# First layer of a four-branch mixer: its start cut into four steps by feature rows, with fp32 modulation weights as the stationary operand

## The chip, the cores and the metric

The kernel runs on one core of one Trainium2 chip. The metric is the device time of one launch in microseconds (us); lower is better. Before the change three runs gave 2394.82, 2383.02 and 2387.49 us: median 2387.49.

## The reference

Two layers (DEPTH = 2) of one mixer work on 1024 latent tokens and 256 context tokens of 1024 features. Cut to the part that the change touches:

```python
shift, scale, gate = jnp.split(c_act @ w_ada[l] + b_ada[l], 3, axis=-1)     # the same with c_ctx for the context
h  = _rmsnorm(x, norm_g[l]) * (1.0 + scale[:, None]) + shift[:, None]
hc = _rmsnorm(xc, norm_g[l]) * (1.0 + scale_c) + shift_c
ckv, krope, u_s5, x_lru, cq, x_pool, gpath, mlogit = jnp.split(h @ w_in[l], IN_SPLITS, axis=-1)
... four token mixers (latent attention, S5, RG-LRU, pooling), gates, merge, w_out ...
x = x + gate[:, None] * y
```

The modulation is a vector-matrix product for two vectors (latent and context) with the 1024 x 2048 part of `w_ada` that holds shift and scale. Every column of every input product needs all 1024 feature rows of `h`, and row k of `h` needs the modulation of feature tile k and the root mean square of its token, which is a sum over all features of `x`.

## The kernel before

Features lie on partitions, tokens on the free axis, in three chunks: 0 (256 context tokens), 1 and 2 (512 latent tokens each). The eight feature tiles of 128 are the index k. Large products run in float32r: `split` makes a high and a low part of each operand (ScalarE copies the rounded high part, VectorE or GpSimd subtracts), and `gemm` runs three passes per k (lo*hi, hi*lo, hi*hi) into one PSUM bank, so a column tile of one chunk costs 24 matmuls.

The start of the first layer (`run`, L1151) follows the steps of the string `START` (L43): load x by chunk (x), squares and root mean squares (q, `stats`), modulation of 256 features (a, `ada_first`, L258), and two input rows of one chunk (b, or p with a part on GpSimd; `build_h`, L314). `ada_first` splits each 128 x 512 piece of `w_ada` into two float32r parts (`wah`, `wal`) and streams them, 256 columns at a time, past a stationary operand of 4 columns (`chl`, both vectors in two parts); the 4 x 256 result is copied out by ScalarE and turned by two transposes, then VectorE adds bias and gain (`ada_end`):

```python
for d in range(2):
    for w in (lo, hi):
        self.mm(pt, self.cact[:, k + d], w[:, 256 * d:256 * d + 256], k + d == 0 and w is lo, k + d == NK - 1 and w is hi)
```

`mla_in` (L345) then multiplies all three chunks by column tiles 0 (`ckv`) and `w_kr` (`krope`), in the banks pg, pg, pS, pS, pS, pm. After it come `mla_kv`, `s5_in` (the first PSUM tile of which is a product of chunk 0 in pg), `lru_in` (L560: column tiles 3 and 4 of all chunks), `cq_in` and the rest.

A scheduler sets the order of each engine's instructions when the kernel is built, by data dependences, by the order of the code and by the priorities that `hp()` raises. On the chip each engine runs its own list in that fixed order, and an instruction that waits holds up all that stand behind it on its engine. All transfers are issued from one queue (SP), also in a fixed order. PSUM pools: `psg` 2 banks, `pss` 3, `psm` 2, `psp` 1; a bank is given again once its last reader is done.

Of the kernel before, what the change touches and what calls it, by code (L numbers as in the profile page):

```python
# [35 lines left out]
SC = 192  # chunk columns of the S5 recurrence: ctx 32, latent 128, ctx again 32  # L36
# [31 lines left out]
class Net:  # L68
# [75 lines left out]
    def rsqrt(self, y, v, t):  # L144
        """y = v ** -0.5 by Newton's steps from the exponent-halving guess."""
# [16 lines left out]
    def load_w(self, src, nk, small=False):  # L162
        """[128, nk * m] stationary columns -> per k the high and low tiles, loaded in parts of at most 512 columns."""
# [28 lines left out]
    def prologue(self):  # L192
# [5 lines left out]
        self.dma(self.ident, I["ident"])  # L198
# [13 lines left out]
        self.qmask = [k[:, 5:6], k[:, 6:7]]  # rows of q without the copies of the rope part  # L212
        self.vec = []
        for l in range(DEPTH):
            a = self.t(pk, f"vec{l}", NV)
            self.dma(a, I["vec"][l])
            self.vec.append(a)
        self.mod = [view(self.t(pk, f"mod{l}", 48), 24, 2) for l in range(DEPTH)]
        cv, t = self.t(pk, "cv", 16), self.sc(16)
        self.cv = view(cv, 8, 2)  # L220
        self.dma(cv, I["cvec"])
        self.act(t, cv, AF.Tanh, scale=0.5)
        self.stt(cv, t, 1.0, cv, ALU.add, ALU.mult)
        ch = view(self.t(pk, "chl", 32, dt=F32R), 8, 4)
        self.split(ch[:, :, 0:2], ch[:, :, 2:4], view(cv, 8, 2))
        self.cact = ch
# [51 lines left out]
    def ada_end(self, l, f, n, pq, rest=None):  # L278
        """Modulation of feature tiles f .. f + n - 1 from its products (the sum of pq and rest): bias, and the norm's gain on 1 + scale."""
# [4 lines left out]
        if rest is not None:  # L284
            self.stt(mo, rest, 0.5, mo, ALU.mult, ALU.add)
# [4 lines left out]
    def stats(self, ci, parts, pool, R):  # L290
        """Reciprocal root mean squares of the tokens of chunk ci, on all partitions of R, from squares [128, n].

        A generator: sums and roots, then the spread to the partitions.
        """
# [16 lines left out]
        self.act(R[:, s0:s0 + n], pr[:, 0:n], AF.Copy)  # L311
        yield

    def build_h(self, l, ci, x, R, ks, pool=False):  # L314
        """Rows ks of the normalised, modulated input of chunk ci (high and low parts)."""
        s0, n = CH[ci]
        who = 1 if ci == 0 else 0
        for k in ks:
# [4 lines left out]
            if pool:  # L323
                self.act(tmp, x[:, k], AF.Identity, scale=A)
                self.tt(tmp, tmp, R[:, s0:s0 + n], ALU.mult, self.nc.gpsimd)
            else:
                self.stt(tmp, x[:, k], A, R[:, s0:s0 + n], ALU.mult, ALU.mult)
# [4 lines left out]
    def tok_sums(self, out, parts, ones):  # L332
        """Sums over features (partitions) of parts [K, n] -> out [128 tokens, n / 128 (, cols)]."""
# [11 lines left out]
    def mla_in(self, l, pa):  # L345
        """Columns ckv and krope, scaled by their norms' gains; sums of squares by token."""
# [989 lines left out]
```

## Time and profile before

| what | value |
|---|---|
| runs: lowest, median, highest | 2383.02, 2387.49, 2394.82 us |
| span of the profiled execution | 2395.9 us |
| TensorE matmul busy over the span | 2303.0 us (96%) |
| VectorE, ScalarE, GpSimd busy | 1585.0, 989.4, 223.3 us |
| moved by DMA | 234.52 MB, mean 98 GB/s |

The page gives no time of the profiled execution beside its span of 2395.9 us, which is its own time here; it lies 8.4 us above the median of the runs. In a row of a timeline the first number is the start in us from the begin of the span, the second the time until the end of the group. Matmuls are pipelined, so their duration holds a latency; how long one occupies the engine is read from one start to the next. A float32 matmul (not float32r) shows as two rows: a group "x8" of 128x2 stands for four matmuls of the program.

### The profile page before, as it was taken

Reading aid. Unit: us, or ns where it says so; the run is one execution under the profiler, and the core shown is the slowest. Engines: PE = TensorE matmul, PEld = TensorE weight load, DVE = VectorE, ACT = ScalarE, POOL = GpSimd, SP = SyncE. Lnnn points to the kernel's source line nnn. Section 1 sums busy time; section 2 is a strip of 40 time slices with the busy share of each in tenths; the row PEclk is TensorE's granted clock in tenths of the full one; section 3 lists DMA queues with packets and bytes.
Section 4 is the critical chain, followed back from the end, with each engine's and each line's share of the span. In section 5 each row is a group of like instructions: output and inputs, shape, how many; then the busy total and the mean of one; then the engine's idle time right before and its main releaser. Section 6 shows DMA issues by size and latency. Waiting matters only on the chain. (4 is left out here: it accounts for less than half of the span.)

```text
span 2395.9 us, 33295 instructions
## 1 busy us (share of the span) xinstructions
PE 2303.0 (96%) x11808; PEld 1883.5 (79%) x11808; DVE 1585.0 (66%) x3533; ACT 989.4 (41%) x1971; POOL 223.3 (9%) x265
## 2 busy tenths in 40 slices
PE   3899999999989999999999999999999999999999
PEld 2687888888778777888888777778888788877887
DVE  6745659766887977445563864679667988864243
ACT  5535656666322222212142444756665322322231
POOL 1200000000000111111112100000000001111110
PEclk8889999999999999999999999999999999999999
DMA  7132241221533324223324423142212431233135
GB/s 248 46 100 67 81 151 55 65 67 49 156 103 99 93 74 126 86 71 111 103 91 132 146 90 110 58 161 70 74 58 80 142 111 49 81 90 102 47 115 158
DMA packets 212455, 234.52 MB, mean 98 GB/s; under 512 B 76352, under 2 KB 138048, under 8 KB 212288
## 3 DMA queue, kind: packets, MB, share of 16 engines
q1 hardware_dynamic: 212288, 232.39, 31.9%
q8 instruction: 93, 1.52, 0.3%
q14 instruction: 74, 0.61, 0.1%
HBM read 173.86 MB, written 58.46 MB: 97 GB/s over the span
## 5 line engine op out<-in xcount | busy, mean ns | idle before, releaser
L139 PE MATMUL pg<-h,wh 128*128 128x512 f32 (+1 forms) x4608 | 1364.1, 377 | 2.9 <-DVE h L124 2.8
L139 PEld LDWEIGHTS pg<-h,wh 128*128 128x128 f32 x4608 | 837.5, 190 | 161.7 <-DVE h L124 5.7
L139 PE MATMUL pg<-h,wl 128*128 128x512 f32 (+2 forms) x2304 | 881.2, 383 | 3.6 <-ACT h L136 3.2
L139 PEld LDWEIGHTS pg<-h,wl 128*128 128x128 f32 (+1 forms) x2304 | 437.4, 190 | 86.1 <-ACT h L136 5.0
L121 DVE TENSOR_TENSOR wl<-wr,wh 128x512 fp32r<-128x512 f32 x268 | 193.2, 723 | 194.6 <-ACT wh L136 193.8
L136 ACT ACTIVATE wh<-wr 128x512 fp32r<-128x512 f32 x268 | 168.2, 628 | 296.5 <-PE pg L139 157.2
L136 ACT ACTIVATE st<-pg 128x512 f32<-128x512 f32 (+1 forms) x200 | 110.7, 554 | 335.9 <-PE pg L139 333.7
L121 POOL TENSOR_TENSOR y<-y,st 128x512 f32<-128x512 f32 (+1 forms) x120 | 151.0, 1258 | 971.4 <-DVE st L124 930.1
L139 PE MATMUL pm<-b,wph 128*128 128x512 f32 (+1 forms) x640 | 185.3, 373 | 1.6 <-DVE b L121 1.6
L136 ACT ACTIVATE P<-pS,sm,qs 128x512 f32<-128x512 f32 (+1 forms) x200 | 138.7, 703 | 48.0 <-DVE sm L128 44.9
L124 DVE SCALAR_TENSOR_TENSOR st<-st,pm 128x512 f32<-128x512 f32 (+1 forms) x120 | 75.5, 630 | 121.4 <-PE pm L139 111.9
L139 PE MATMUL pS<-k,q 128*128 128x512 f32 (+1 forms) x600 | 144.3, 364 | 1.9 <-DVE q L121 1.7
L139 PEld LDWEIGHTS pm<-b,wph 128*128 128x128 f32 x640 | 116.0, 189 | 25.0 <-DVE b L121 3.1
L139 PE MATMUL pP<-pt,v 128*128 128x256 f32 x656 | 127.7, 301 | 3.4 <-DVE pt L121 1.3
L139 PEld LDWEIGHTS pP<-pt,v 128*128 128x128 f32 x656 | 99.6, 188 | 35.9 <-ACT pt L136 22.3
L527 DVE TENSOR_REDUCE sm<-pS 128x1 f32<-128x512 f32 (+1 forms) x200 | 113.3, 586 | 15.8 <-PE pS L139 14.5
L121 DVE TENSOR_TENSOR pt<-pm,pt 128x512 fp32r<-128x512 f32 x164 | 106.9, 682 | 25.0 <-ACT pt L136 24.3
L139 PE MATMUL pm<-b,wpl 128*128 128x256 f32 (+1 forms) x320 | 119.9, 375 | 2.5 <-DVE y L124 1.8
L136 ACT ACTIVATE pt<-pm 128x512 fp32r<-128x512 f32 x164 | 91.2, 600 | 70.6 <-PE pm L142 70.4
L139 PEld LDWEIGHTS pS<-k,q 128*128 128x128 f32 x600 | 98.8, 189 | 19.0 <-ACT P L136 4.3
L142 PE MATMUL pm<-ident,P 128*128 128x128 f32 x656 | 107.1, 274 | 0.2 <-ACT P L136 0.2
L124 DVE SCALAR_TENSOR_TENSOR pP<-wa,cv,pP 128x256 f32<-128x256 f32 x196 | 95.4, 487 | 15.1 <-DMA wa<-in_w_ada 11.0
(240 smaller groups left out, 2637.7 us busy)
## 6 DMA issues: line engine op xcount, KB each, us to landing
wr<-in_w_in SPq DMA_DIRECT2D x196, 256.0 KB, 2.9
wa<-in_w_ada SPq DMA_DIRECT2D x96, 256.0 KB, 2.9
wr<-in_w_out SPq DMA_DIRECT2D x64, 256.0 KB, 3.0
gD<-st SPq DMA_DIRECT2D x32, 256.0 KB, 2.0
tD<-st SPq DMA_DIRECT2D x32, 256.0 KB, 2.1
og<-oD SPq DMA_DIRECT2D x32, 256.0 KB, 2.8
og<-gD SPq DMA_DIRECT2D x32, 256.0 KB, 3.1
wr<-in_w_branch SPq DMA_DIRECT2D x64, 128.0 KB, 2.1
```

The costliest lines, as they stand in the source:

```text
L121: (eng or self.nc.vector).tensor_tensor(out=out, in0=a, in1=b, op=op)
L124: self.nc.vector.scalar_tensor_tensor(out=out, in0=a, scalar=s, in1=b, op0=op0, op1=op1)
L136: self.nc.scalar.activation(out=out, in_=a, func=func, scale=scale, **kw)
L139: self.nc.tensor.matmul(out=out, lhsT=lhsT, rhs=rhs, start=start, stop=stop)
L142: self.nc.tensor.transpose(out=out, in_=in_, identity=ident)
L527: nc.vector.tensor_reduce(out=mx3[:, i:i + 1], in_=S, axis=AX.X, op=ALU.max)
```

## The change

- `START` and the loop over it are gone. `start` takes their place, in a priority raised by 30000.
- The prologue's small loads (`cvec`, `ident`, `vec`) are issued behind the first quarter of chunk 1's x.
- `ada_first` no longer splits `w_ada`. The raw float32 weights, 128 x 128 at a time, are the stationary operand, and the two vectors `cv[:, k]` stream past them (2 columns): 32 matmuls per 256 features, with no copy and no transpose behind them.
- Four steps s = 0 to 3: modulation of feature tiles 2s and 2s + 1; rows 2s and 2s + 1 of `h` for chunk 1; then the three passes of these two rows for four column tiles (`ckv`, `krope`, and the two of the RG-LRU, tiles 3 and 4) of chunk 1. These four sums stay in two pg and two pS banks over all steps. The weights of a step come in slices of two feature tiles (`slices`).
- The raw weights of steps 0 and 2 lie in the place of chunk 2's x, those of steps 1 and 3 in a buffer of their own; the weight slices of steps 0 and 1 lie in the place of chunk 0's x. Chunks 2 and 0 of x are therefore loaded behind step 2's modulation weights, and their squares, statistics and rows come after step 3.
- `mla_in` takes chunk 1's two results from the held banks (`pre`), `lru_in` the other two (`lru_pad` copies them into the padded input).
- `R` is one tile per chunk instead of one for all.

```diff
-START = "x2 x1 a0 x0 q1 a1 q2 q0 a2 b01 p02 b00 b11 p12 p21 b10 b22 a3 b20 b31 p32 b30"
...
-    def ada_first(self, i, pool):
-        for c in (i // 2, 2 + i // 2):
-            cols = slice(256 * (i % 2), 256 * (i % 2) + 256)
-            bank = self.pP()
-            pt, pq = bank[0:4, 0:256], bank[:, 256:264]
+    def ada_load(self, i, raws):
+        cols = slice(256 * (i % 2), 256 * (i % 2) + 256)
+        raws = view(raws, 16, 256)
+        for j, c in enumerate((i // 2, 2 + i // 2)):
             for k in range(0, NK, 2):
-                raw, hi, lo = self.t(pool, "wa", 512, 8), self.t(pool, "wah", 512, 4, F32R), self.t(pool, "wal", 512, 4, F32R)
-                self.dma(view(raw, 2, 256), self.I["w_ada"][0, c, k:k + 2].rearrange("k p n -> p k n")[:, :, cols])
-                self.split(hi, lo, raw, self.nc.gpsimd if i > 0 and k < 4 else None)
-                for d in range(2):
-                    for w in (lo, hi):
-                        self.mm(pt, self.cact[:, k + d], w[:, 256 * d:256 * d + 256], k + d == 0 and w is lo, k + d == NK - 1 and w is hi)
-            row = self.st()
-            self.act(row[0:4, 0:256], pt, AF.Copy)
+                self.dma(raws[:, 8 * j + k:8 * j + k + 2], self.I["w_ada"][0, c, k:k + 2].rearrange("k p n -> p k n")[:, :, cols])
+        return raws
+    def ada_first(self, i, raws):
+        pq = view(self.pP(), 2, 2, 2)
+        for c in range(2):
             for t in range(2):
-                self.tr(pq[:, 4 * t:4 * t + 4], row[0:4, 128 * t:128 * t + 128], self.ident[0:4, 0:4])
-            pq = view(pq, 2, 4)
-            self.ada_end(0, 4 * c + 2 * (i % 2), 2, pq[:, :, 0:2], pq[:, :, 2:4])
+                for k in range(NK):
+                    self.mm(pq[:, c, t], raws[:, 8 * c + k, 128 * t:128 * t + 128], self.cv[:, k], k == 0, k == NK - 1)
+            self.ada_end(0, 8 * c + 2 * i, 2, pq[:, c])
...
-        for part, ci in [(0, 1), (1, 1), (0, 0), (1, 0), (0, 2), (1, 2)] if l > 0 else [(p, ci) for p in range(2) for ci in (1, 2, 0)]:
+        for part, ci in [(0, 1), (1, 1), (0, 0), (1, 0), (0, 2), (1, 2)] if l > 0 else [(0, 1), (1, 1), (0, 2), (1, 2), (0, 0), (1, 0)]:
...
-            ps = self.hgemm(ws[part], ci, 64 if part else 128, next(bank)())
+            ps = pre.pop(part) if ci == 1 and part in pre else self.hgemm(ws[part], ci, 64 if part else 128, next(bank)())
...
+    def start(self, pd, wa):
...
+        w01, a0 = self.t(pd, "x0", 2048), self.t(pd, "x2", 4096)
...
+        for k in range(0, NK, 2):
+            self.dma(xs[1][:, k:k + 2], I["xT"][:, k:k + 2, s0:s0 + n])
+            if k == 0:
+                self.prologue_rest()
...
+        raws = self.ada_load(0, a0)
+        for _ in self.stats(1, [self.squares(1, xs[1], pd)], pd, R):
+            pass
+        banks = [self.pg(), self.pg(), self.pS(), self.pS()]
+        for s in range(4):
+            self.ada_first(s, raws)
+            self.build_h(0, 1, xs[1], R, (2 * s, 2 * s + 1))
+            if s < 3:
+                ws[s + 1] = self.slices(s + 1, (w01, w23)[(s + 1) // 2][:, 1024 * ((s + 1) % 2):1024 * ((s + 1) % 2) + 1024])
+                raws = self.ada_load(s + 1, a1 if s == 0 else self.t(wa, "wa", 4096) if s == 2 else self.t(pd, "x2", 4096))
+            if s == 2:
+                load(2)
+                load(0)
+            for f in range(4):
+                m = 64 if f == 1 else 128
+                for d in range(2):
+                    k = 2 * s + d
+                    xh, xl = self.Hh[:, k, s0:s0 + n], self.Hl[:, k, s0:s0 + n]
+                    hi, lo = ws[s][f][d]
+                    for i, (a, b) in enumerate(((lo, xh), (hi, xl), (hi, xh))):
+                        self.mm(banks[f][0:m, 0:n], a, b, k == 0 and i == 0, k == NK - 1 and i == 2)
+        for ci in (2, 0):
+            for _ in self.stats(ci, [self.squares(ci, xs[ci], pd)], pd, R):
+                pass
+            for k in range(0, NK, 2):
+                self.build_h(0, ci, xs[ci], R, (k, k + 1), k == 4)
+        return {f: banks[f][0:64 if f == 1 else 128, 0:n] for f in range(4)}
```

Where the instructions stand now. A row is the line in the source, the operation, its output, its inputs and its size; x30 means that so many alike follow each other. First TensorE at the first product of the input projection. Before, the modulation of 256 features (`pP`, from the parts `wal` and `wah`) runs between the first and the later products of `ckv` (`pg`):

```order
L139 MATMUL pP_506<-wal_539,chl_109 4x256
L139 MATMUL pP_506<-wah_538,chl_109 4x256
L142 MATMUL pP_506<-ident_85,st_547 128x4 x2
L139 MATMUL pg_792<-h_84,wl_776 128x512
L139 MATMUL pP_624<-wal_627,chl_109 4x256
```

Now, from the end of step 0 to the begin of step 1 (`pP_290` is the modulation of step 1, `pP_380` that of step 2; `pg_197`, `pg_198`, `pS_199` and `pS_200` are the held banks):

```order
L135 MATMUL pS_200<-h_84,wh_137 128x512 x2
L135 MATMUL pS_200<-h_84,wl_138 128x512
L135 MATMUL pS_200<-h_84,wh_137 128x512 x2
L135 MATMUL pP_290<-cv_90,wa_115 128x2 x30
L135 MATMUL pg_197<-h_84,wl_248 128x512
L135 MATMUL pg_198<-h_84,wl_248 64x512
L135 MATMUL pS_199<-h_84,wl_255 128x512
L135 MATMUL pS_200<-h_84,wl_255 128x512
L135 MATMUL pP_380<-cv_90,x_347 128x2 x2
L135 MATMUL pg_197<-h_84,wh_247 128x512 x2
```

All 30 products of a step's modulation stand behind all products of the step before, and the step's own products behind them.

The second place is TensorE at the statistics of chunks 2 and 0 (`pm`: sums of squares, then the transposes of the roots). Before, they stand among the modulation's products:

```order
L142 MATMUL pP_459<-ident_85,st_500 128x4
L142 MATMUL pm_409<-ident_85,rv_407 128x128 x4
L139 MATMUL pm_438<-const_87,acc_415 128x1 x2
L142 MATMUL pP_459<-ident_85,st_500 128x4
L139 MATMUL pP_506<-wal_509,chl_109 4x256
```

Now they stand behind the last product of step 3, with no other product between them; the first product of chunk 0 (`pS_831`) follows:

```order
L135 MATMUL pS_200<-h_84,wh_433 128x512 x2
L135 MATMUL pS_200<-h_84,wl_434 128x512
L135 MATMUL pS_200<-h_84,wh_433 128x512 x2
L135 MATMUL pm_567<-const_91,acc_544 128x1 x4
L138 MATMUL pm_586<-ident_85,rv_584 128x128 x4
L135 MATMUL pm_649<-const_91,acc_626 128x1 x2
L138 MATMUL pm_666<-ident_85,rv_664 128x128 x2
L135 MATMUL pS_831<-h_84,wl_727 128x256
```

The third place is ScalarE at the squares of chunk 2. Before, they (`sq` of `x_121`) stand among the high parts of the modulation weights:

```order
L136 ACTIVATE sq_384<-x_121 128x512
L136 ACTIVATE wah_304<-wa_303 128x512
L136 ACTIVATE wah_321<-wa_320 128x512
L136 ACTIVATE R_119<-pm_266 128x512
L136 ACTIVATE wah_331<-wa_330 128x512
```

Now the squares of chunk 2 (`x_446`) begin behind step 3's two rows of `h`:

```order
L132 ACTIVATE wh_433<-ws_116 128x512
L132 ACTIVATE h_84<-st_420,mod_88 128x512
L132 ACTIVATE h_84<-st_512,mod_88 128x512
L132 ACTIVATE h_84<-st_516,mod_88 128x512
L132 ACTIVATE acc_544<-x_446 128x512
L132 ACTIVATE sq_546<-x_446 128x512
```

No square of chunks 2 and 0 stands ahead of step 3 any more.

## Rows read from the trace of the kernel before

**Rows 1.** Page, part 1: busy time, share of the span and instructions, TensorE first.

```profile
PE 2303.0 (96%) x11808; PEld 1883.5 (79%) x11808; DVE 1585.0 (66%) x3533; ACT 989.4 (41%) x1971; POOL 223.3 (9%) x265
```

**Rows 2.** Waits of TensorE, 0 to 110 us: total, times, longest.

```profile
PE pP L139 <- DVE wal L121: 27.5, 4, 26.8
```

**Rows 3.** Windows: length, busy by engine, granted clock, DMA share, GB/s.

```profile
0.00:10.00 10.00, 0.00 (x0) 0.00 (x0) 2.14 (x14) 2.95 (x5) 0.20 (x4) 1.00 0.74 232
10.00:20.00 10.00, 0.00 (x0) 0.00 (x0) 1.37 (x2) 1.26 (x2) 0.00 (x0) 1.00 0.90 301
...
0.00:110.00 110.00, 66.60 (x334) 42.86 (x335) 78.22 (x166) 61.64 (x115) 29.58 (x32) 0.89 0.48 155
110.00:114.00 4.00, 4.00 (x23) 2.91 (x22) 2.29 (x10) 2.34 (x5) 0.00 (x0) 1.00 0.34 105
115.00:135.00 20.00, 20.00 (x73) 17.42 (x73) 6.08 (x46) 5.55 (x12) 0.00 (x0) 0.50 0.00 0
110.00:300.00 190.00, 188.64 (x957) 153.26 (x956) 104.36 (x206) 99.45 (x158) 0.38 (x6) 0.95 0.25 82
```

**Rows 4.** TensorE's timeline, 67 to 71 us: start, duration, instruction, idle.

```profile
66.97 0.68 PE L139 MATMUL pg<-h,wl 128*128 128x512 f32 x1 [1.93 <-ACT h L136]
67.44 0.41 PE L139 MATMUL pP<-wal,chl 128*4 128x256 f32 x1
...
70.60 0.28 PE L139 MATMUL pP<-wah,chl 128*4 128x256 f32 x1
```

**Rows 5.** TensorE's timeline, 124 to 151 us: products of two columns.

```profile
124.19 1.70 PE L139 MATMUL pP<-const,sc 128*128 128x2 f32 x8
125.75 0.56 PE L139 MATMUL pg<-h,wh 128*128 128x256 f32 x1
...
150.24 1.02 PE L139 MATMUL pP<-const,sc 128*128 128x2 f32 x8
151.12 0.37 PE L139 MATMUL pg<-h,wh 128*128 128x256 f32 x1
```

**Rows 6.** TensorE's timeline, 130 to 144 us: products of 512 columns.

```profile
130.17 1.05 PE L139 MATMUL pg<-h,wh 128*128 128x512 f32 x2
131.02 0.63 PE L139 MATMUL pg<-h,wl 128*128 128x512 f32 x1
...
143.24 0.63 PE L139 MATMUL pg<-h,wh 128*128 128x512 f32 x2
143.71 0.39 PE L139 MATMUL pg<-h,wl 128*128 128x512 f32 x1
```

**Rows 7.** TensorE's timeline, 110 to 112 us: products of 256 columns.

```profile
110.05 0.28 PE L139 MATMUL pg<-h,wl 128*128 128x256 f32 x1
110.17 0.40 PE L139 MATMUL pg<-h,wh 128*128 128x256 f32 x2
110.40 0.28 PE L139 MATMUL pg<-h,wl 128*128 128x256 f32 x1
...
111.57 1.55 PE L139 MATMUL pS<-lat,sel 64*128 64x256 f32 x4
```

**Rows 8.** Timeline of three engines, 95 to 99 us: modulation to input row.

```profile
95.54 0.28 PE L142 MATMUL pP<-ident,st 4*128 4x4 f32 x2
...
97.06 1.42 DVE L124 SCALAR_TENSOR_TENSOR st<-x,mod,R 128x512 f32<-128x512 f32 x2
...
97.85 1.39 ACT L136 ACTIVATE h<-st,mod 128x512 fp32r<-128x512 f32 x2
```

**Rows 9.** Timeline of two engines: squares, statistics and a 256-column row.

```profile
21.62 1.13 ACT L136 ACTIVATE sq<-x 128x512 f32<-128x512 f32 x2
...
59.93 0.16 DVE L128 TENSOR_SCALAR nsm<-pm 128x2 f32<-128x2 f32 x1 [0.65 <-PE pm L139]
...
62.16 0.29 DVE L307 COPY rv<-nsm 128x256 f32<-128x256 f32 x1
...
88.88 0.48 DVE L124 SCALAR_TENSOR_TENSOR h<-st,mod,h 128x256 fp32r<-128x256 f32 x1
```

More of the change, by code (lines that the diff above doesn't have):

```diff
@@ L197, in prologue @@
         self.ident = self.t(pk, "ident", 128)
-        self.dma(self.ident, I["ident"])
+        self.vec = [self.t(pk, f"vec{l}", NV) for l in range(DEPTH)]
+        self.mod = [view(self.t(pk, f"mod{l}", 48), 24, 2) for l in range(DEPTH)]
+        self.cv = view(self.t(pk, "cv", 16), 8, 2)
         k = self.t(pk, "const", 16)
@@ L212, in prologue, with prologue_rest @@
         self.qmask = [k[:, 5:6], k[:, 6:7]]
-        self.vec = []
-        for l in range(DEPTH):
[L215 to L226, printed above, removed]
+    def prologue_rest(self):
+        cv, t = self.cv, self.sc(16)
+        flat = cv.rearrange("p a b -> p (a b)")
+        self.dma(flat, self.I["cvec"])
+        self.dma(self.ident, self.I["ident"])
+        for l in range(DEPTH):
+            self.dma(self.vec[l], self.I["vec"][l])
+        self.act(t, flat, AF.Tanh, scale=0.5)
+        self.stt(flat, t, 1.0, flat, ALU.add, ALU.mult)
     def ada(self, l, i, bank):
@@ L283, in ada_end @@
         self.stt(mo, pq, 0.5, col(V_BADA + f), ALU.mult, ALU.add)
-        if rest is not None:
-            self.stt(mo, rest, 0.5, mo, ALU.mult, ALU.add)
         if 8 <= f < 16:
@@ L310, in stats @@
             self.tr(pr[:, t * 128:(t + 1) * 128], rv[:, t], self.ident)
-        self.act(R[:, s0:s0 + n], pr[:, 0:n], AF.Copy)
+        self.act(R[ci], pr[:, 0:n], AF.Copy)
         yield
@@ L343, in tok_sums, with mla_in @@
         self.nc.vector.tensor_copy(out=out, in_=src)
-    def mla_in(self, l, pa):
+    def mla_in(self, l, pa, pre):
         I, vec = self.I, self.vec[l]
@@ L557, in attention, with lru_pad, lru_in @@
                 self.dma(oD[h // 2, (h % 2) * 64:(h % 2) * 64 + 64, q0:q0 + 256], ov[0:64, 1])
-    def lru_in(self, l, pa):
+    def lru_pad(self, pa, ps=None):
+        xp = self.t(pa, "xp", 1312, 2)
+        for c in (0, 258, 259, 1285):
+            self.nc.gpsimd.memset(xp[:, c:c + (2 if c in (0, 259) else 1)], 0.0)
+        if ps is not None:
+            with self.hp():
+                self.act(xp[:, 261:773], ps, AF.Copy)
+        return xp
+    def lru_in(self, l, pa, pads):
         vec, out = self.vec[l], []
@@ L565, in lru_in @@
             w = self.load_w(self.I["w_in"][l, 3 + f], NK)
-            xp = self.t(pa, "xp", 1312, 2)
-            for c in (0, 258, 259, 1285):
-                self.nc.gpsimd.memset(xp[:, c:c + (2 if c in (0, 259) else 1)], 0.0)
-            for ci in range(3):
+            xp = pads[f] if pads else self.lru_pad(pa)
+            for ci in ((0, 2) if pads else range(3)):
                 s0, n = CH[ci]
@@ L1072, in next_h @@
     def next_h(self, l, xs, acc, pd):
-        R = self.t(pd, "R", NT)
+        R = {ci: self.t(pd, f"R{ci}", CH[ci][1]) for ci in range(3)}
         for cis in ((1, 0), (2,)):
@@ L1119, in out_proj, with layer @@
                         self.dma(self.x1D[:, :, s0:s0 + n], xs[ci])
-    def layer(self, l):
+    def layer(self, l, pre):
         tc = self.tc
@@ L1126, in layer @@
         with self.phase("pr") as pr, self.phase("pa") as pa:
-            m = self.mla_in(l, pa)
+            m = self.mla_in(l, pa, pre)
+            pads = [self.lru_pad(pa, pre[2 + f]) for f in range(2)] if pre else None
             self.mla_kv(l, m, pa)
             uF, uD = self.s5_in(l, pr)
-            xl = self.lru_in(l, pa)
+            xl = self.lru_in(l, pa, pads)
             self.lru(l, xl, oD[LRUB], lat, pa, pr)
@@ L1149, in layer, with squares, slices @@
                 self.merge(l, lat, oD, gD, tD, pc, s5)
+    def squares(self, ci, x, pd):
+        n = CH[ci][1]
+        a = self.t(pd, "acc", 512, 2)[:, 0:n]
+        for k in range(NK):
+            sq = a if k == 0 else self.t(pd, "sq", 512, 2)[:, 0:n]
+            self.act(sq, x[:, k], AF.Square)
+            if k > 0:
+                self.tt(a, a, sq, ALU.add)
+        return a
+    def slices(self, s, raws):
+        w_in, out = self.I["w_in"][0], []
+        for kind in range(2):
+            raw = view(raws[:, 512 * kind:512 * kind + 512], 2, 2, 128)
+            if kind == 0:
+                self.dma(raw[:, 0], view(w_in[0], 8, 128)[:, 2 * s:2 * s + 2])
+                self.dma(raw[:, 1, :, 0:64], view(self.I["w_kr"][0], 8, 64)[:, 2 * s:2 * s + 2])
+            else:
+                self.dma(raw, w_in[3:5].rearrange("f p (k m) -> p f k m", m=128)[:, :, 2 * s:2 * s + 2])
+            hi, lo = (view(self.whl.tile([128, 512], F32R, tag=t, name=self.name(t)), 2, 2, 128) for t in ("wh", "wl"))
+            for f, m in enumerate((128, 64) if kind == 0 else (256,)):
+                p = (lambda a: a[:, f, :, 0:m]) if kind == 0 else (lambda a: a)
+                self.split(p(hi), p(lo), p(raw))
+            for f in range(2):
+                m = 64 if kind == 0 and f == 1 else 128
+                out.append([(hi[:, f, d, 0:m], lo[:, f, d, 0:m]) for d in range(2)])
+        return out
@@ new lines, in start, with load @@
+    def start(self, pd, wa):
+        I = self.I
+        R, xs = {}, {}
+        w01, a0 = self.t(pd, "x0", 2048), self.t(pd, "x2", 4096)
+        for ci in (0, 2, 1):
+            R[ci] = self.t(pd, f"R{ci}", CH[ci][1])
+        xs[1] = view(self.t(pd, "x1", 4096), 8, 512)
+        a1, w23 = self.t(wa, "wa", 4096), self.t(wa, "ws", 2048)
+        def load(ci):
+            s0, n = CH[ci]
+            xs[ci] = view(self.t(pd, f"x{ci}", 8 * n), 8, n)
+            for k in range(0, NK, 4):
+                self.dma(xs[ci][:, k:k + 4], I["xT"][:, k:k + 4, s0:s0 + n])
+        s0, n = CH[1]
+        for k in range(0, NK, 2):
+            self.dma(xs[1][:, k:k + 2], I["xT"][:, k:k + 2, s0:s0 + n])
+            if k == 0:
+                self.prologue_rest()
+        ws = [self.slices(s, (w01, w23)[s // 2][:, 1024 * (s % 2):1024 * (s % 2) + 1024]) if s == 0 else None for s in range(4)]
+        raws = self.ada_load(0, a0)
[25 more added lines that the diff above has]
+        return {f: banks[f][0:64 if f == 1 else 128, 0:n] for f in range(4)}
@@ L1156, in run @@
         pd = pd_.__enter__()
-        xs = {}
-        with self.tc.tile_pool(name="wa", bufs=1, reuse_waits="tile") as wa:
-            R = self.t(pd, "R", NT)
-            for ci in (1, 2, 0):
-                n = CH[ci][1]
-                xs[ci] = view(self.t(pd, f"x{ci}", 8 * n), 8, n)
-            for step in START.split():
-                op, ci = step[0], int(step[-1])
-                s0, n = CH[ci % 3]
-                if op == "x":
-                    for k in (0, 4):
-                        self.dma(xs[ci][:, k:k + 4], I["xT"][:, k:k + 4, s0:s0 + n])
-                elif op == "a":
-                    self.ada_first(ci, wa)
-                elif op == "q":
-                    a = self.t(pd, "acc", 512, 2)[:, 0:n]
-                    for k in range(NK):
-                        sq = a if k == 0 else self.t(pd, "sq", 512, 2)[:, 0:n]
-                        self.act(sq, xs[ci][:, k], AF.Square)
-                        if k > 0:
-                            self.tt(a, a, sq, ALU.add)
-                    for _ in self.stats(ci, [a], pd, R):
-                        pass
-                else:
-                    k = 2 * int(step[1])
-                    self.build_h(0, ci, xs[ci], R, (k, k + 1), op == "p")
+        with self.hp(30000), self.tc.tile_pool(name="wa", bufs=1, reuse_waits="tile") as wa:
+            pre = self.start(pd, wa)
         for l in range(DEPTH):
@@ L1187, in run @@
             pd_.__exit__(None, None, None)
-            self.layer(l)
+            self.layer(l, pre if l == 0 else {})
             pd_ = self.phase("pd")
```

6 lines of the change are left out of this document (3 added, 3 removed).

## The prediction, as it was put down before the run

> **What bounds the kernel now.** I read the page's busy times first: TensorE is busy for 2303.0 of 2395.9 us [rows 1]. The windows then show where it is not. From 110 us on it works 188.64 of 190 us; in the first 110 us only 66.60 [rows 3]. So a change in the start is worth what it does to the moment from which TensorE has unbroken work, and to the work that is left then. The list of waits shows what made TensorE late: 26.8 us until the first low part of the modulation weights is there [rows 2].
>
> I use one mark for both kernels: the first product of `s5_in` (chunk 0, pg), which stands behind `mla_in`. Before, it starts at 110.05 us [rows 7]. Behind it lies the same work in both, with two exceptions: the changed kernel has already made column tiles 3 and 4 of chunk 1 (2 x 24 = 48 products of 512 columns), and three of the six groups of `mla_in`'s token sums where before had made two.
>
> **Prices.** Starts divided by counts. A product of 512 columns occupies TensorE (131.02 - 130.17) / 2 = 0.425 us in one stretch and (143.71 - 143.24) / 2 = 0.235 us in another [rows 6]. The granted clock is 0.50 from 115 to 135 us and 1.00 from 110 to 114 [rows 3]: the levels of 1.2 and 2.4 GHz. One of 256 columns costs 0.115 us at the upper level [rows 7]; I take 0.23 at the lower. The new modulation products have the very form of `mla_kv`'s token sums, 128 x 128 float32 stationary and two columns moving, and these show two passes per matmul: (125.75 - 124.19) / 8 = 0.195 us a pass at the lower level, (151.12 - 150.24) / 8 = 0.11 at the upper [rows 5].
>
> Which level holds? TensorE restarts after a wait at 66.97 us with 256-column products of 0.41 us, and they are at 0.28 from 70.60 on [rows 4]: 3.6 us of dense products before the rise. At 111.57 begins a stretch of products with a 64-row `sel` and of token sums [rows 7], and the clock falls between 114 and 115 us, though TensorE stays busy: it is busy for all 20.00 us of the low stretch [rows 3]. So I let a dense block begin at the lower level and run 5 us before it rises (3.6 seen, and a step's block has four thin passes near its begin), and a run of thin products keep the upper level for 3.4 us and then lose it.
>
> The Trainium skill ("TensorE: Matmul & The Clock Gate", LDWEIGHTS) gives a weight load as columns / 1.2 ns, 107 ns for 128, whatever the clock. The row at the upper level agrees (0.11), that at the lower does not (0.195). By the page's figure, an estimate, the thin products would cost some 13 us less and the forecast would be about 2398; the rows decide.
>
> **Part by part.**
>
> Removed: 128 modulation products of 4 x 256, 16 transposes, and the split of `w_ada` (32 copies on ScalarE at about 0.56 us [rows 9], 32 subtractions on VectorE and GpSimd). ScalarE and VectorE get free, but TensorE becomes what they wait for, so I take nothing for it beyond the new chain itself.
>
> Step 0. Before its modulation is complete, 2.1 MB of x, 0.14 MB of small tables, 0.46 MB of slices and 2.1 MB of `w_ada` must land. At the transfer rates seen (232 GB/s in the first 10 us, then 301 [rows 3]) x and the slices are in at 11.3 us and the two halves of `w_ada` at 14.8 and 18.2. The last square and sum end near 11.4, the sums over partitions near 13; the roots take 62.16 + 0.29 - 59.93 = 2.5 us [rows 9], so the spread is ready by 17. The 64 thin passes at the lower level: the last loaded piece of the first half and its second tile end at 18.7, four transposes make it 19.8, the second half's 32 x 0.195 = 6.2 make it 26.0. Thin products decide here, not DMA.
>
> Steps 0 to 2, each: TensorE ends the modulation; VectorE makes bias and gain and the scaled row, ScalarE the high part. Before, from the transposes at 95.54 + 0.28 to the first high part at 97.85 + 0.70 it takes 2.7 us [rows 8], with two other VectorE rows between; I take 2.3. TensorE does nothing in this gap, since the next step's modulation stands behind the products that wait. The dense block of 24 products: 5 us at 0.425 (11.8 products), 12.2 at 0.235 = 2.9, and four thin passes 0.8: 8.7. Then 60 thin passes of the next step: 31 in the first 3.4 us, 29 x 0.195 = 5.7, and 0.4 where VectorE reads the first half of the bank: 9.5. Sum 2.3 + 8.7 + 9.5 = 20.5 us, three times 61.5. Step 3 has the gap and a block without thin passes: 2.3 + 7.9 = 10.2. Chunk 1 is done at 26.0 + 61.5 + 10.2 = 97.7 us. Bounds per step: all at the upper level 15.3 us (2.3 + 24 x 0.235 + 64 x 0.11 + 0.4), all at the lower 25.4.
>
> The tail. Chunk 2's x waits for step 2's modulation (near 67 us) and has over 20 us to arrive: hidden behind step 2's products and step 3. Its squares stand on ScalarE behind step 3's rows, 8 x 0.56 = 4.5 us beside step 3's products: hidden too, and 4.5 us if they are late. After 97.7: sums over partitions 0.9; the roots 2.5 with 3 us of other VectorE rows in between (six sums for chunk 0 and two weight splits); transposes and copy of R 1.7: R is there at 105.8. VectorE then makes 14 rows of 512 columns at 0.71 [rows 8] = 9.9, 14 of 256 at 0.45 (0.48 alone [rows 9]) = 6.3, and chunk 0's roots 2.5: 124.5 us. TensorE has almost nothing in all this: its list has chunk 0 next, which is made last. Then the held banks are read (1.0), and until the mark TensorE has 12 products of 256 columns at the lower level 2.8, eight thin passes 1.6, 24 of 512 in 7.9, 24 at the upper level 5.6, two groups of sums 1.8 and 12 of 256 in 1.4: 22.1 in all. The mark is at 146.6 us.
>
> The sum: 146.6 - 110.05 = 36.5 us later, less 48 x 0.235 = 11.3 of work done ahead, less one group of sums 1.6: 23.6, taken as 24 us slower. The profiled execution would have 2395.9 + 24 = 2420; on the median of the runs, 2387.5 + 24 = 2411 (rounded down).
>
> At no cost: the small loads and 12 slice transfers on SP (it waits for thin products most of the time; if not, some 5 us of issue); the splits of the slices (ScalarE and VectorE are idle beside the thin products); the two copies into the padded input (one PSUM read each, counted above as 1.0). What follows the mark I take as unchanged, the low stretch after it (20.4 us at half clock) included; it could go or double, 10 us either way.
>
> **Rivals.**
>
> A, the upper level throughout the start. If TensorE rises in step 0 and thin products hold it, step 0 ends at 20.4 (bound by the second half's landing at 18.2), three steps take 45.9 and step 3 7.9: 74.2; the tail to 124.5's place is 26.8: 101.0; the rest 17.7: 118.7. That is 8.7 later, less 11.3 and 0.9: 3.5 us faster, 2384. For it: TensorE never idles long in a step. Against it: 20.00 busy us at a granted clock of 0.50 [rows 3]. The Trainium skill says for the clock (same page, "What's actually happening") that "activity releases the throttle"; read so that any busy engine is active, this is A, and the trace speaks against that reading.
>
> B, faster: the low stretch after the mark does not come back. In the changed kernel the mark follows dense products and three of six sum groups are already gone; if the clock then holds through `mla_kv`, 20.4 us of low level turn into 10.2. It decides only on top of A's start: 2384 - 10 = 2374. Against it: `sel` and the token sums stand there in about the same density.
>
> C, slower still: the dense blocks never rise. Every step costs 25.4, step 3 12.5, and the tail's two blocks of 24 rise by 7 us: 15 + 2 + 7 = 24 more, 2435. For it: 115 to 135 us holds dense products too, for 10 us at the lower level. Against it: 3.6 us sufficed at 67.
>
> **How the numbers follow.** The forecast (2397 to 2428) 0.64, A 0.17, B 0.10, C 0.09. A measurement can tell 0.5%, 12 us, from no change: faster is below 2375.5, slower above 2399.4. Faster: most of B and a little of A, 0.11. Same: the rest of A and of B, and the forecast's low end, 0.19. Slower: the rest of the forecast and C, 0.70. The range reaches from A to short of C, 2386 to 2430; the likeliest case alone has 2397 to 2428.
>
> **What would show it.** In the profile after: thin passes near 0.195 us and a granted clock of 0.50 in the second half of each run of them; four dense blocks with 2 to 3 us of idle TensorE ahead of each; chunk 1 done between 90 and 105 us; then 20 us or more in which TensorE is nearly idle and VectorE makes rows; the mark near 147 us. I am wrong if the granted clock is 1.00 throughout the steps (A), if thin passes take markedly less than 0.11 us, if the rows of chunks 2 and 0 take VectorE much less than 19 us, or if the time after the mark differs by more than 10 us between the kernels.

## The result: 1.2% slower, 28.5 us, as forecast in kind and 4.5 us more in size

Four runs of the changed kernel gave 2416.16 to 2421.34 us, median 2417.8. The kernel before had a median of 2389.3 beside them (2383.02 to 2394.82). The ratio is 1.0123, 95% interval 1.0100 to 1.0147. The forecast was 2411, with a range of 2386 to 2430.

TensorE's busy time grew by 17.4 us; that of VectorE, ScalarE and GpSimd shrank by 18 to 24 each [rows 1]:

```profile
PE 2320.4 (96%) x11920; PEld 1913.6 (79%) x11920; DVE 1566.9 (65%) x3520; ACT 971.3 (40%) x1938; POOL 199.4 (8%) x249
```

TensorE's waits in the changed kernel, 0 to 160 us (total, times, longest). The 26.8 us at the start for the split weights [rows 2] are gone; 13.6 us for the first sums of squares are left of them. New are four gaps for ScalarE's high part and 19 us for the reciprocal roots of chunks 2 and 0:

```profile
PE pm L138 <- DVE rv L298: 19.0, 2, 13.7
PE pm L135 <- DVE acc L117: 13.6, 1, 13.6
PE pg L135 <- ACT h L132: 8.1, 4, 2.1
```

TensorE's timeline in the changed kernel (start, duration, instruction; in brackets the idle time ahead of it and what ended it): the two halves of the modulation of step 0, the first 512-column product, one whole step from 52.75 to 73.58 (24 products, 28 and 32 passes of two columns, the gap), the end of chunk 1, the two waits behind it, and the mark, the first `s5_in` product [rows 7]:

```profile
15.31 6.96 PE L135 MATMUL pP<-cv,x 128*128 128x2 f32 x32
...
23.03 6.83 PE L135 MATMUL pP<-cv,x 128*128 128x2 f32 x32
31.93 1.22 PE L135 MATMUL pg<-h,wl 128*128 128x512 f32 x2 [2.07 <-ACT h L132]
...
52.75 1.22 PE L135 MATMUL pg<-h,wl 128*128 128x512 f32 x2 [1.99 <-ACT h L132]
...
61.77 3.18 PE L135 MATMUL pP<-cv,x 128*128 128x2 f32 x28
65.21 6.38 PE L135 MATMUL pP<-cv,x 128*128 128x2 f32 x32 [0.25 <-DVE mod L120]
73.58 1.22 PE L135 MATMUL pg<-h,wl 128*128 128x512 f32 x2 [1.99 <-ACT h L132]
...
102.66 0.95 PE L135 MATMUL pm<-const,acc 128*128 128x1 f32 x8
108.88 1.12 PE L138 MATMUL pm<-ident,rv 128*128 128x128 f32 x4 [5.27 <-DVE rv L298]
...
124.36 0.66 PE L138 MATMUL pm<-ident,rv 128*128 128x128 f32 x2 [13.72 <-DVE rv L298]
126.55 0.58 PE L135 MATMUL pS<-h,wl 128*128 128x256 f32 x1 [1.53 <-ACT h L132]
...
150.65 0.28 PE L135 MATMUL pg<-h,wl 128*128 128x256 f32 x1
```

Windows of the changed kernel (columns as in [rows 3]; the number behind POOL's is the granted clock). The first two windows of 0.50 are each the second half of a run of two-column passes with the gap and the first half of the block behind it; the last is the stretch of `sel` products and token sums behind `mla_in`:

```profile
46.00:58.00 12.00, 10.01 (x37) 8.56 (x37) 4.20 (x9) 1.85 (x3) 0.00 (x0) 0.50 0.51 154
60.00:64.00 4.00, 4.00 (x30) 3.63 (x28) 0.00 (x0) 0.54 (x2) 0.00 (x0) 1.00 0.00 0
66.00:78.00 12.00, 10.01 (x39) 8.84 (x39) 4.20 (x9) 1.85 (x3) 0.00 (x0) 0.50 0.43 155
80.00:86.00 6.00, 5.75 (x41) 5.12 (x40) 0.16 (x1) 0.00 (x0) 0.00 (x0) 1.00 0.54 180
...
102.00:127.00 25.00, 4.48 (x23) 3.63 (x21) 20.97 (x52) 13.12 (x25) 2.83 (x2) 0.60 0.29 98
...
156.00:170.00 14.00, 14.00 (x52) 11.80 (x53) 3.75 (x23) 3.95 (x8) 0.00 (x0) 0.50 0.00 0
```

A second mark, the first softmax instruction of the first layer's attention, lies behind all reordering; its row is one of a tile's view (durations min/median/max, first and last start). The kernel before, then the changed one:

```profile
L136 ACT ACTIVATE P<-pS,sm,qs x200: 552/774/800, 346.0 to 1833.6; 128x512 f32<-128x512 f32 x64, 128x256 f32<-128x256 f32 x36
```

```profile
L132 ACT ACTIVATE P<-pS,sm,qs x200: 554/775/799, 375.2 to 1851.0; 128x512 f32<-128x512 f32 x64, 128x256 f32<-128x256 f32 x36
```

It starts 29.2 us later. The profiled spans differ by only 18.4, because the profiled execution of before (span 2395.9) is one of its longer ones: it is slower in later stretches that the change does not touch. Between 595 and 903 us, for one, it needs 308 us at a mean clock of 0.96, where the changed kernel needs 303 at 0.98 for the same work (624 to 927). The medians, 28.5 apart, agree with the second mark. I use that mark for all experiments.

### The profile page after: what moved, and what is told of

It reads as the page before. It is cut to its first block, busy times and chain, and to the rows that moved or that the text cites. A ratio compares the mean times of both kernels' runs of the same rounds, so it can differ in the third digit from the quotient of the medians.

```text
span 2414.3 us, 33411 instructions
## 1 busy us (share of the span) xinstructions
PE 2320.4 (96%) x11920; PEld 1913.6 (79%) x11920; DVE 1566.9 (65%) x3520; ACT 971.3 (40%) x1938; POOL 199.4 (8%) x249
## 5 line engine op out<-in xcount | busy, mean ns | idle before, releaser
L521 DVE TENSOR_REDUCE sm<-pS 128x1 f32<-128x512 f32 (+1 forms) x200 | 113.3, 586 | 15.8 <-PE pS L135 14.9
```

Of the source, the lines that this page charges most:

```text
L521: nc.vector.tensor_reduce(out=mx3[:, i:i + 1], in_=S, axis=AX.X, op=ALU.max)
```

## Experiments

In the table, "chunk 1" is the time at which the last product of chunk 1 in the held banks is done; "softmax" is the second mark. Each ratio is to runs of the kernel before on the same chip.

| kernel | median us | ratio to before, 95% | chunk 1 | softmax |
|---|---|---|---|---|
| changed | 2417.8 | 1.0123 (1.0100 to 1.0147) | 102.7 | 375.2 |
| e1_early | 2392.8 | 1.0026 (1.0009 to 1.0044) | 105.6 | 352.7 |
| e2_among | 2419.9 | 1.0145 (1.0120 to 1.0170) | 103.5 | 375.6 |
| e3_eighth | 2378.1 | 0.9953 (0.9932 to 0.9974) | 62.1 | 330.7 |
| e4_alone | 2406.5 | 1.0083 (1.0061 to 1.0104) | | 363.3 |
| e5_split | 2392.0 | 0.9995 (0.9978 to 1.0013) | 95.7 | 346.6 |
| e6_vec | 2379.6 | 0.9946 (0.9925 to 0.9968) | 84.6 | 336.9 |
| e7_alonevec | 2373.4 | 0.9938 (0.9923 to 0.9953) | | 327.3 |
| e8_nopool | 2377.9 | 0.9955 (0.9932 to 0.9978) | 84.0 | 331.0 |
| e9_aftervec | 2390.6 | 1.0004 (0.9987 to 1.0021) | 80.9 | 347.9 |
| e10_wide | 2394.5 | 1.0010 (0.9995 to 1.0025) | 84.1 | 348.4 |

### The tail taken away

```diff
-        w01, a0 = self.t(pd, "x0", 2048), self.t(pd, "x2", 4096)
+        a0 = self.t(wa, "wb", 4096)
...
-            if s == 2:
+            if s == 0:
                 load(2)
                 load(0)
...
+            for ci in ((2, 0)[s - 1],) if s in (1, 2) else ():
+                for _ in self.stats(ci, [self.squares(ci, xs[ci], pd)], pd, R):
+                    pass
+            for ci, ks in ((), (), ((2, (0, 2)),), ((2, (4,)), (0, (0, 2, 4)), (2, (6,)), (0, (6,))))[s]:
+                for k in ks:
+                    self.build_h(0, ci, xs[ci], R, (k, k + 1), k == 4)
```

> The changed kernel with the tail of its start taken away: the weight slices go through the stream's own two buffers, so chunks 2 and 0 of x have their place from the beginning, are loaded during step 0, and their squares, sums, roots and rows are made in steps 1 to 3 instead of behind them. Theory A (the added time is the low-clock thin products in the steps plus the wait for VectorE behind them): TensorE's idle stretches 103.6 to 108.9 and 110.6 to 126.55 (20.6 us without the one group in between) go, the products before the first s5_in product start near 103 instead of 126.55, the mark comes at about 128 to 131 instead of 150.65, and the time is about 2395 (2391 to 2400). Rival B (the end of the start is not what sets the time: later waits take the place of the idle time): 2410 to 2418. Rival C (VectorE cannot make the rows beside the steps: step period grows over 22 us): 2400 to 2412.

The time fell by 25 us (23 by the ratios). TensorE in e1_early, from the end of chunk 1 (105.59) through two short waits to the mark (136.11):

```profile
105.59 0.28 PE L135 MATMUL pS<-h,wl 128*128 128x256 f32 x1
...
109.15 0.39 PE L135 MATMUL pS<-h,wl 128*128 128x256 f32 x1 [1.28 <-ACT h L132]
...
112.15 0.58 PE L135 MATMUL pS<-h,wl 128*128 128x256 f32 x1 [1.97 <-ACT h L132]
...
136.11 0.39 PE L135 MATMUL pg<-h,wl 128*128 128x256 f32 x1
```

So the idle 20 us went, and A held over B. But the mark moved by 14.5 us only, not by the 20 or more that I expected: step 3 ends 2.9 later, and the products behind it wait 3.3 and run partly at the lower level. The other 8 us of the 22.5 at the softmax lie behind the mark. There the low stretch, 156 to 171 us in the changed kernel, is missing; the same `sel` products and token sums run at the upper level:

```profile
135.00:155.00 20.00, 19.70 (x116) 15.24 (x115) 8.99 (x41) 9.66 (x21) 0.00 (x0) 1.00 0.10 33
```

### The gaps filled

```diff
+        self.ada_first(0, raws[0])
         for s in range(4):
-            self.ada_first(s, raws)
             self.build_h(0, 1, xs[1], R, (2 * s, 2 * s + 1))
...
+            if s < 3:
+                self.ada_first(s + 1, raws[s + 1])
```

> The changed kernel with the modulation of step s+1 made ahead of and among the 512-column products of step s (both matrices are loaded a step earlier), the tail as it is. Theory A1 (thin products keep the lower level whatever stands beside them, .15 us a pass on average): only the gaps of 2.0 us ahead of three or four blocks go; chunk 1 is done near 95, the time is 2409 to 2412. Theory A2 (the level falls because thin products run alone for 9 us; between 512-column products it stays at the upper one): a pass takes .11, a 512-column product .235, a step 12.7 instead of 20.8, chunk 1 is done near 75 to 85, the granted clock is 1.00 from step 1 on, and the time is 2392 to 2400. Rival B (start not on the path): 2415 to 2420.

Both A1 and A2 failed: 2419.9. That lies in B's range, but not for B's reason: chunk 1 was done no earlier, so this run does not test whether the start sets the time (e1_early does). TensorE's waits for `h` in pg fell from 8.1 us (4 times) to 2.3 (2 times), yet chunk 1 is done at 103.5. TensorE in e2_among, first a window, then products among passes:

```profile
60.00:100.00 40.00, 37.72 (x133) 31.57 (x134) 10.35 (x22) 7.11 (x13) 0.00 (x0) 0.50 0.27 92
```

```profile
86.87 0.85 PE L135 MATMUL pP<-cv,wa 128*128 128x2 f32 x4
87.58 1.20 PE L135 MATMUL pS<-h,wh 128*128 128x512 f32 x2
88.58 0.63 PE L135 MATMUL pS<-h,wl 128*128 128x512 f32 x1
89.00 0.63 PE L135 MATMUL pS<-h,wh 128*128 128x512 f32 x1
89.43 4.26 PE L135 MATMUL pP<-cv,wa 128*128 128x2 f32 x20
```

With the passes strewn among them the 512-column products do not get the clock up: it is 0.50 for 40 us, a product costs (89.00 - 88.58) = 0.42, a pass (4.26 / 20) 0.21. What the gaps gave back, the blocks lost. This is rival C's mechanism, reached by another order.

### Most of the thin products left out

```diff
-                for k in range(NK):
-                    self.mm(pq[:, c, t], raws[:, 8 * c + k, 128 * t:128 * t + 128], self.cv[:, k], k == 0, k == NK - 1)
+                self.mm(pq[:, c, t], raws[:, 8 * c, 128 * t:128 * t + 128], self.cv[:, 0])
```

> The changed kernel with seven eighths of the thin products left out: only the first of the eight row tiles goes into the modulation (its values are not the reference's). All loads, waits, rows and 512-column products stay. Theory A: each thin run of 9.4 shrinks to 1.2, so four runs give back about 33 us and the time is 2385; where the granted clock also stays at the upper level between the blocks, a block is 5.7 to 7 instead of 9, some 8 more, 2377. Rival D (the steps are set by the loads of 2.2 MB each or by VectorE's rows, not by TensorE): steps stay above 15 us and the time above 2395.

39.8 us less by time (2378.1, A's second case), 44.5 at the softmax; a step is 53.61 - 43.28 = 10.3 us, and the loads do not hold it, so D is out:

```profile
43.28 1.22 PE L135 MATMUL pg<-h,wl 128*128 128x512 f32 x2 [1.99 <-ACT h L132]
...
53.61 1.22 PE L135 MATMUL pg<-h,wl 128*128 128x512 f32 x2 [1.99 <-ACT h L132]
```

### One part alone: the kernel before with the new modulation

```diff
-                    self.split(hi, lo, raw, self.nc.gpsimd if i > 0 and k < 4 else None)
-                    for d in range(2):
-                        for w in (lo, hi):
-                            self.mm(pt, self.cact[:, k + d], w[:, 256 * d:256 * d + 256], ...)
+        for c in range(2):
+            for t in range(2):
+                for k in range(NK):
+                    self.mm(pq[:, c, t], raws[:, 8 * c + k, 128 * t:128 * t + 128], self.cv[:, k], ...)
```

> One part of the change alone: the kernel before with its order of the start, its mla_in and its pads, but with the fp32 modulation (128 weight columns stationary, two vectors moving, no splits). Theory A: the splits (20 on VectorE of .85, 12 on GpSimd of 1.45, 32 on ScalarE of .62) and the wait of 26.8 us for them go; 256 thin passes at .11 to .213 take 28 to 54 us on TensorE, partly at the lower level. The first s5_in product comes at 85 to 105 instead of 110, the time is 2368 to 2385 by the median of the kernel before of 2389. Rival E (the thin products by themselves carry the loss: at the lower level they hold TensorE until past 110): 2389 to 2400.

I expected a gain and got a loss: 17 us at the softmax, 18 by the medians. E's mechanism was right (the first `s5_in` product comes at 131.5), but at 2406.5 the time lies above the 2389 to 2400 that E gave. So a loss by these passes does not need the steps. In e4_alone the scheduler puts products of `mla_in` among the passes. They take 74.19 - 73.77 = 0.42 us as long as passes stand among them, and (113.15 - 112.69) / 2 = 0.23 only behind the last run:

```profile
73.77 0.63 PE L139 MATMUL pg<-h,wl 128*128 128x512 f32 x1
74.19 0.63 PE L139 MATMUL pg<-h,wh 128*128 128x512 f32 x1
...
103.10 4.26 PE L139 MATMUL pP<-cv,wa 128*128 128x2 f32 x20
...
112.69 0.62 PE L139 MATMUL pS<-h,wh 128*64 128x512 f32 x2
113.15 0.63 PE L139 MATMUL pg<-h,wh 128*128 128x512 f32 x2
```

### The modulation of before in the steps, and fp32 with the vectors standing still

Both on e1_early. e5_split has the 4-column vectors, the splits and 32 float32r products a step again:

```diff
-            self.ada_first(s, raws)
+            self.ada_first(s, wa)
...
+                    self.split(hi, lo, raw, self.nc.gpsimd if i > 0 and k < 4 else None)
+                    for d in range(2):
+                        for w in (lo, hi):
+                            self.mm(pt, self.cact[:, k + d], w[:, 256 * d:256 * d + 256], ...)
```

> As e1_early (2392.8 us), with the modulation made as in the kernel before: the two vectors, in a high and a low part, stand still as 4 columns, the weights are split on ScalarE, VectorE and GpSimd and pass as 256 float32r columns, 32 products a step instead of 64 passes of 2 columns. Theory A (2-column fp32 products hold TensorE and keep its clock at the lower level, also for the blocks behind them): the granted clock is 1.00 in most of the steps, a product takes .14 to .24, a block of 24 near 6, a step 13 to 17 instead of 20.8, chunk 1 is done at 75 to 90 instead of 102.7, the time is 2365 to 2382. Rival F (the splits, 8 of 512 columns a step at .85 on VectorE or 1.45 on GpSimd, hold the steps as they held the kernel before, 26.8 us of wait): steps of 20 or more, 2390 or more. Rival G (the level falls in any stretch in which 512-column blocks pause, whatever stands between): blocks of 9 and steps of 19, about 2386.

By ratio it gained some 7 us over e1_early (0.9995 against 1.0026), 6.1 at the softmax, less than A wanted; the medians, from two chips, are only 0.8 apart. Chunk 1 is done 10 us earlier, but TensorE waits some 12.5 us for the copies, splits, sums and roots around them, and 2392.0 lies in F's range, though its steps are uneven (25.7, 17.9 and 14.0 us). The longest such groups of its waits, 0 to 150 us:

```profile
PE pP L135 <- DVE sc L117: 4.3, 3, 2.2
PE pP L138 <- ACT st L132: 3.1, 6, 0.7
PE pP L135 <- DVE wal L117: 2.9, 2, 1.5
```

e6_vec only swaps the operands:

```diff
-            for t in range(2):
-                for k in range(NK):
-                    self.mm(pq[:, c, t], raws[:, 8 * c + k, 128 * t:128 * t + 128], self.cv[:, k], ...)
+            for k in range(NK):
+                self.mm(pt[:, 256 * c:256 * c + 256], self.cv[:, k], raws[:, 8 * c + k], ...)
+        self.act(row[0:2], pt, AF.Copy)
+        for c in range(2):
+            for t in range(2):
+                self.tr(pq[:, c, t], row[0:2, 256 * c + 128 * t:256 * c + 128 * t + 128], self.ident[0:2, 0:2])
```

> As e1_early (2392.8 us), with the modulation still in fp32 and without splits, but the two vectors stationary and the weights moving: 16 products of 256 fp32 columns in two passes each a step, then four small transposes by way of ScalarE. Only which operand stands still is changed. Theory A (it is the 2 columns that keep the clock low): the granted clock stays at 1.00 in the runs of such passes and in the blocks behind them; a pass of 256 fp32 columns takes .3 to .38 at that level (the kernel before has 377 ns for 256-column fp32 rows elsewhere), so 32 passes are 10 to 12, a block 5.7 to 7, a step 18 to 20 with its gaps: 2380 to 2390. Rival G (any modulation between the blocks lets the level fall): a pass .5 to .7, a run of 16 to 22, steps near 30, time above 2420.

This gained 13 us over e1_early by the medians, 19 by the ratios and 15.8 at the softmax. A 256-column fp32 pass takes 0.22 us at the upper level, less than my 0.3 to 0.38, and the clock stays up from the first block to 73 us, as A wanted; G is out. The window (columns as in [rows 3]):

```profile
40.00:74.00 34.00, 30.73 (x144) 16.11 (x142) 20.45 (x61) 13.89 (x27) 0.00 (x0) 1.00 0.36 114
```

### The same swap alone, in the changed kernel and in the kernel before

The edit is e6_vec's, made in the changed kernel (e9_aftervec) and in e4_alone (e7_alonevec).

> The changed kernel with one edit: the two vectors stationary and the weights moving in the fp32 modulation; chunks 2 and 0 wait behind the steps as in the changed kernel. Theory A (two separate prices that add up, the 2-column passes and the tail): what this edit gave from e1_early to e6_vec (13 us) it gives here too, 2402 to 2407, with steps near 16 to 17, chunk 1 done near 86 to 90 and the idle time behind it as long as before (about 20 us). Rival J (they overlap: the loads of chunks 2 and 0 and their squares come no earlier, so the tail grows by what the steps lose): 2412 or more.

> As e4_alone (the kernel before with fp32 modulation without splits, 2406.5 us), with the vectors stationary and the weights moving as in e6_vec. Theory A (of the one part alone, it was the 2-column passes at the lower level that made it slower, and not that the splits are gone): 128 passes of .22 take 28 us of TensorE, VectorE loses 17 us of splits, the first s5_in product comes at 82 to 98 instead of 110, time 2362 to 2378. Rival H (VectorE's squares, roots and rows, over 60 us of work ahead of that product, set it in any case): 2382 to 2392.

In e9_aftervec the whole loss of the change is gone: 27 us, twice what I expected from e1_early to e6_vec. Neither A's sum nor J fits. A step is 14.8 us (43.48 to 58.30), 6 less; chunk 1 is done at 80.9; behind it TensorE still waits 14.3 and 1.5. To the end of chunk 1 the swap gave the same both times, 21.8 here and 21.0 from e1_early to e6_vec. Here the tail shrank too: chunk 2's roots are made during step 3, and the first wait (5.27) is gone, so the mark comes 28.3 earlier (122.4). Together the two edits move the mark by 36.7 us (e6_vec: 113.9), 6 less than 14.5 and 28.3. The rest of the difference between 25 + 27 = 52 and the 38 us that e6_vec gained over the changed kernel lies mostly behind the mark, where e6_vec has a low stretch and e1_early has none: 223.0 and 216.6 us from there to the softmax. A run of 24 passes and the first passes and products of the next step:

```profile
43.48 0.73 PE L135 MATMUL pg<-h,wl 128*128 128x512 f32 x2
...
49.26 5.34 PE L135 MATMUL pP<-x,cv 128*2 128x256 f32 x24
...
56.48 1.89 PE L135 MATMUL pP<-wa,cv 128*2 128x256 f32 x8 [0.25 <-DVE mod L120]
58.30 0.73 PE L135 MATMUL pg<-h,wl 128*128 128x512 f32 x2
...
59.58 0.40 PE L135 MATMUL pg<-h,wl 128*128 128x512 f32 x1
```

e7_alonevec has the lowest median, 16 us below before, and lies in A's range, so H is out; its first `s5_in` product comes at 102.5, later than the 82 to 98 expected. The splits are gone, and TensorE begins at 22.3 us instead of 26.8. Held banks and steps are not needed for this gain. The best stepped kernels (e8_nopool with a median 4.5 us higher, e6_vec with a ratio of 0.9946) are not clearly behind it: the intervals overlap.

### Rows without GpSimd

```diff
-                    self.build_h(0, ci, xs[ci], R, (k, k + 1), k == 4)
+                    self.build_h(0, ci, xs[ci], R, (k, k + 1))
```

> As e6_vec (2379.6 us), with rows 4 and 5 of chunks 2 and 0 made on VectorE as the others instead of by way of GpSimd. Theory A: TensorE's two waits of 1.0 and 2.0 us ahead of rows 4 and 5 of chunk 0 go, and with them most of the low stretch that follows (88 to 99 in e6_vec): 2372 to 2377. Rival I (VectorE, busy 9.7 of 10 us there, takes 2.4 us more, so the same wait stands one row later): 2379 to 2383.

Against e6_vec the ratio to before did not fall (0.9955 and 0.9946, intervals overlapping), though this profile has the softmax 5.9 us earlier. Of the two waits ahead of chunk 0's rows (they stand at rows 5 and 6 of 0 to 7, not at 4 and 5 as I had read), that of row 5 (1.0 us) is gone, that of row 6 stays, at 1.76. A and I are not told apart.

### More work on TensorE

```diff
-        pq = view(self.pP(), 2, 2, 2)
+        pq = view(self.pP(), 2, 2, 2, 32)
...
-                    self.mm(pq[:, c, t], raws[...], self.cv[:, k], ...)
+                    self.mm(pq[:, c, t], raws[...], bc(col3(self.cv[:, k]), [128, 2, 32]), ...)
```

> The changed kernel with one edit that only adds work to TensorE: in the fp32 modulation the weights stay stationary and the number of products stays, but each vector is passed 32 times over (64 columns instead of 2; one of the 32 copies is used). Theory A (the weights standing still cost .11 a pass at the upper level as at any small width; what makes them dear is the lower level into which the 2-column runs let TensorE fall): with 64 columns the level stays up, a pass stays near .11 to .12, a block of 24 takes 5.7 to 6, a step about 15, chunk 1 is done near 82 to 86, and the time is 2388 to 2398. Rival K (it is the change of the stationary matrix in every pass that costs .2 a pass, or the level falls whenever it changes that often): passes of .2 or more, steps of 20.8 or more, 2416 or more.

The same number of passes with the same stationary weights, each 64 columns wide instead of 2, and the kernel is 23 us faster by the medians, 27 by the ratios and at the softmax. TensorE in e10_wide, passes of step 0, one step (50.15 to 63.80, 13.65 us) and a window:

```profile
22.91 7.09 PE L135 MATMUL pP<-cv,x 128*128 128x64 f32 x32 [0.26 <-DVE mod L120]
...
50.15 0.71 PE L135 MATMUL pg<-h,wl 128*128 128x512 f32 x2
...
55.80 0.55 PE L135 MATMUL pP<-cv,x 128*128 128x64 f32 x4
56.61 3.79 PE L135 MATMUL pP<-cv,x 128*128 128x64 f32 x32 [0.26 <-DVE mod L120]
60.65 3.34 PE L135 MATMUL pP<-cv,wa 128*128 128x64 f32 x28 [0.26 <-DVE mod L120]
63.80 0.71 PE L135 MATMUL pg<-h,wl 128*128 128x512 f32 x2
64.34 0.63 PE L135 MATMUL pS<-h,wl 128*128 128x512 f32 x2
```

```profile
40.00:74.00 34.00, 32.73 (x232) 29.14 (x230) 12.80 (x25) 10.09 (x18) 0.00 (x0) 1.00 0.52 171
```

From the modulation of step 1 to that of step 3 a pass is 3.79 / 32 = 0.12, where the changed kernel has 0.11 for its first 28 and 6.38 / 32 = 0.20 for the next 32. In step 0, at the lower level, it is 7.09 / 32 = 0.22, as with two columns. K is out: the change of weights costs no more than 0.12 a pass with the clock up. The scheduler here also puts 28 passes of the next step ahead of a block, which fills the gap: 2.0 of the 7.2 us that a step gained are that gap, so the width is not all of the 23 us. e2_among shows that such an order alone gives nothing at the lower level.

## Why the prediction was right, point by point

**The bound.** Right: the second mark is 29.2 us later and the medians 28.5, so what the start lost is the loss. The first mark gives nearly the same: 150.65 - 110.05 = 40.6, less 11.3 and 1.6 of work done ahead is 27.7. Against the 36.5 of the forecast it is 4.1 later, 3.9 of them by step 0.

**Step 0.** Missed by 3.9 us: it ends near 29.9, not 26.0. A pass at the lower level costs 6.96 / 32 = 0.22, not the 0.195 taken from [rows 5], and the statistics' sums began 2.2 us later (13.59 against 11.4), ahead of the passes. The column of the granted clock reads 1.00 there (0.50 first stands in it at 45 us), so I go by the spacing of the passes, 0.22, which is that of the lower level.

**Steps 1 to 3.** Right: gaps of 1.99 us (2.3), blocks of 9.2, 9.0 and 8.9 (8.7), runs of 9.7 to 10.0 (9.5); a step is 20.8 us where 20.5 stood. Chunk 1 is done at 102.7, inside 90 to 105 but 5.0 behind the 97.7, most of it step 0's. That the blocks came out so near was partly luck: they ran some 6 us at the lower level, where I had let them run 5, going by one place of 3.6 us [rows 4].

**The tail.** Right in kind: 19 us of waiting for VectorE. Its rows and roots take from 111.56 to 132.5, 21 us instead of 18.7. TensorE's rest to the mark was shorter (18.2 from 132.5, 22.1 forecast), since chunk 0's products ran while the last rows were made.

**Behind the mark.** Taken as unchanged, and in this pair it nearly was: a low stretch of some 16 us instead of 20.4. That it can go, rival B, was seen in e1_early, where it was worth up to 8 us, and in e7_alonevec. What decides over it stays open: e6_vec has it with the same kinds of products at that place. So that it came back here was partly luck.

**A** was wrong for this kernel (the granted clock fell to 0.50 in every run of passes), and e10_wide shows about what it would have been: a ratio of 1.0010, some 2.4 us slower than before where I gave 3.5 faster, since its step 0 still runs at the lower level and chunk 1 is done at 84.1, not 74.2. (Its 2384 lay just below the range, which was meant to reach it.) **C** was wrong for the blocks as ordered and right for e2_among. The Trainium skill ("TensorE: Matmul & The Clock Gate", LDWEIGHTS) gives a weight load as columns / 1.2 ns, 107 ns for 128, with no clock beside it. The passes here meet that at the upper level only: 0.11 to 0.12 us there, 0.20 to 0.22 at the lower one. Its phrase "activity releases the throttle" (same page, "What's actually happening") does not hold here in the sense that any busy engine is active: in e2_among TensorE was busy for 37.72 of 40 us at 0.50.

## What to carry to other kernels

Price a small matmul by both levels of the clock, and then price its neighbours too: the thin fp32 passes cost the changed kernel some 10 us a step, and slowed the 24 large products behind them from 0.235 to 0.42 for half a block. When a product of a matrix and one or two vectors must run between large ones, let the vectors stand still and the matrix move; here that was worth 13 to 19, 27 and 33 us in three kernels. Look for the stage that is late next before adding gains: tail and operand swap gave 25 and 27 us alone, 38 together (by the medians).

## What the runs showed of the hardware

- Passing each vector 32 times over made the kernel 23 us faster (e10_wide): from step 1 on its passes of 64 fp32 columns took 0.12 us with the clock at 2.4 GHz, where most of the changed kernel's passes of 2 columns took 0.20 to 0.22 at 1.2 GHz. In step 0, at the lower level, both widths took 0.22.
- A pass of 256 moving fp32 columns against a two-column stationary operand took 5.34 / 24 = 0.22 us at the upper level (e9_aftervec).
- The same stretch of work behind `mla_in` ran at the lower level in the changed kernel (156 to 170 us, 0.50) and at the upper one in e1_early (135 to 155 us, 1.00), about 8 us apart.
